# Add residual and RMSNorm over 65,536 rows: four rows per partition and tile instead of two, scaling traced one tile late, last store in rows

## The chip, the cores and the metric

The kernel runs on one core of a Trainium2 chip; the other cores are idle. Times are device microseconds (us) of that core, medians over repeated executions. A profiled execution gives a span, which is about 2 us shorter than the time of the same run because it counts from the first to the last instruction.

A packet is one record of the DMA trace: here the contiguous run of one partition, moved by one of the core's 16 DMA engines. A load or store of a tile gives each engine 8 of them.

## The reference

The input is 32 x 2048 rows of 2048 float32 numbers (8 KiB a row); x, residual and output are 537 MB each.

```python
z = x + residual
rms = np.sqrt(np.mean(z ** 2, axis=-1, keepdims=True) + eps)
return (z / rms * gamma).astype(np.float32)
```

## The kernel before

A tile has 128 partitions with R rows each. The rows of one partition are neighbours in DRAM, so each partition of a tile is one contiguous run of R x 8 KiB. Loads go out on the sync queue, stores on the scalar queue; VectorE adds and scales, ScalarE squares with a running sum and takes the root. (Lines are left out here; the whole kernel follows.)

```python
R = 2
n_tiles = n_rows // (P * R)                                  # 256
x_t = x_f.rearrange("(n p r) m -> n p r m", p=P, r=R)        # r_t, o_t alike
gamma_tile = singles.tile([P, D], fp32)
nc.sync.dma_start(out=gamma_tile, in_=gamma.partition_broadcast(P))
xio = ctx.enter_context(tc.tile_pool(name="xio", bufs=6))
rio = ctx.enter_context(tc.tile_pool(name="rio", bufs=4))
for i in range(n_tiles):
    x_tile = xio.tile([P, R, D], fp32)
    r_tile = rio.tile([P, R, D], fp32)
    nc.sync.dma_start(out=x_tile, in_=x_t[i])
    nc.sync.dma_start(out=r_tile, in_=r_t[i])
    nc.vector.tensor_add(out=x_tile, in0=x_tile, in1=r_tile)             # L56
    for g in range(R):
        nc.scalar.activation(out=sq_junk, in_=x_tile[:, g, :], func=Square,
                             accum_out=ssq[:, g : g + 1])                # L61
    # ... rms = sqrt(ssq / D + eps) on ScalarE (L69), rstd = 1 / rms on VectorE (L77)
    for g in range(R):
        nc.vector.scalar_tensor_tensor(out=x_tile[:, g, :], in0=x_tile[:, g, :],
            scalar=rstd[:, g : g + 1], in1=gamma_tile, op0=mult, op1=mult)  # L80
    nc.scalar.dma_start(out=o_t[i], in_=x_tile)
```

Of the kernel before, what the change touches and what calls it, by code (L numbers as in the profile page):

```python
# [1 line left out]

# [4 lines left out]


@with_exitstack  # L10
def kernel(
    ctx: ExitStack,
    tc: tile.TileContext,
    x: bass.AP,
    residual: bass.AP,
    gamma: bass.AP,
    eps: float,
    out: bass.AP,
):
    nc = tc.nc  # L20
    P = nc.NUM_PARTITIONS
    fp32 = mybir.dt.float32

    x_f = x.flatten_outer_dims()
    r_f = residual.flatten_outer_dims()
    o_f = out.flatten_outer_dims()

    n_rows, D = x_f.shape
    R = 2
    assert n_rows % (P * R) == 0  # L30
    n_tiles = n_rows // (P * R)

    x_t = x_f.rearrange("(n p r) m -> n p r m", p=P, r=R)
    r_t = r_f.rearrange("(n p r) m -> n p r m", p=P, r=R)
    o_t = o_f.rearrange("(n p r) m -> n p r m", p=P, r=R)

    inv_d = 1.0 / float(D)

    singles = ctx.enter_context(tc.tile_pool(name="singles", bufs=1))
    gamma_tile = singles.tile([P, D], fp32)  # L40
    nc.sync.dma_start(out=gamma_tile, in_=gamma.partition_broadcast(P))  # L41
    eps_tile = singles.tile([P, 1], fp32)
    nc.vector.memset(eps_tile, float(eps))  # L43

    xio = ctx.enter_context(tc.tile_pool(name="xio", bufs=6))
    rio = ctx.enter_context(tc.tile_pool(name="rio", bufs=4))
    stats = ctx.enter_context(tc.tile_pool(name="stats", bufs=8))
    psum = ctx.enter_context(tc.tile_pool(name="psum", bufs=1, space=bass.MemoryType.PSUM))

    for i in range(n_tiles):  # L50
        x_tile = xio.tile([P, R, D], fp32)
        r_tile = rio.tile([P, R, D], fp32)
        nc.sync.dma_start(out=x_tile, in_=x_t[i])  # L53
        nc.sync.dma_start(out=r_tile, in_=r_t[i])  # L54

        nc.vector.tensor_add(out=x_tile, in0=x_tile, in1=r_tile)  # L56

        sq_junk = psum.tile([P, D], fp32)
        ssq = stats.tile([P, R], fp32)
        for g in range(R):  # L60
            nc.scalar.activation(  # L61
                out=sq_junk,
                in_=x_tile[:, g, :],
                func=mybir.ActivationFunctionType.Square,
                accum_out=ssq[:, g : g + 1],
            )

        rms = stats.tile([P, R], fp32)
        nc.scalar.activation(  # L69
            out=rms,  # L70
            in_=ssq,
            func=mybir.ActivationFunctionType.Sqrt,
            bias=eps_tile,
            scale=inv_d,
        )
        rstd = stats.tile([P, R], fp32)
        nc.vector.reciprocal(out=rstd, in_=rms)  # L77

        for g in range(R):
            nc.vector.scalar_tensor_tensor(  # L80
                out=x_tile[:, g, :],
                in0=x_tile[:, g, :],
                scalar=rstd[:, g : g + 1],
                in1=gamma_tile,
                op0=mybir.AluOpType.mult,
                op1=mybir.AluOpType.mult,
            )

        nc.scalar.dma_start(out=o_t[i], in_=x_tile)


# [1 line left out]
_INS = ['x', 'residual', 'gamma', 'eps']  # L93
_OUTS = [((32, 2048, 2048), 'float32')]
#: Inputs that are plain numbers.
_NUMBERS = {'eps': 9.999999974752427e-07}


# [26 lines left out]
```

## Time and profile before

| quantity | value | where it is read |
|---|---|---|
| time, median | 3764.7 us (3764.1 to 3765.1) | runs |
| VectorE, ScalarE busy | 62%, 29% | profile page, part 1 |
| DMA busy share; rate | 9 (90% or more) nearly everywhere; 430 to 431 GB/s | page, part 2 |
| usual 16 KiB packet: lasts; start to start on one engine | 611 ns; 607.5 ns | DMA records |
| last load landed; from there to the end of the span | 3740.5 us; 22.0 us | DMA records |

The page of the kernel before. Part 2 cuts the span into 40 slices: busy tenths for each engine and for the DMA engines, then GB/s. Part 3 lists the queues (q1 loads, q10 stores, q14 instruction fetches) with packets, MB and share of the 16 engines' time. Part 4 is the chain of waits that ended last. Part 5 lists groups of instructions: busy us, mean ns of one, and the engine's idle time just before them with what ended most of it.

```profile
span 3762.5 us, 4011 instructions
DVE 2322.1 (62%) x1025; ACT 1103.6 (29%) x1282; POOL 0.2 (0%) x4
...
DMA  9999999999999999999999999999999999999998
GB/s 416 431 430 431 431 430 431 430 431 430 430 431 431 430 431 431 431 431 430 431 431 430 431 431 431 430 431 431 430 431 430 431 431 430 431 430 431 430 431 356
DMA packets 110767, 1611.96 MB, mean 428 GB/s; under 512 B 12304, under 2 KB 12304, under 8 KB 12304
...
q14 instruction: 31, 0.25, 0.0%
...
DMA 91%; DVE 8%; issue 1%; SPq 0%; ACT 0%; DVEq 0%
...
L56 DVE TENSOR_TENSOR x_tile<-x_tile,r_tile 128x4096 f32<-128x4096 f32 x256 | 1132.0, 4422 | 1413.1 <-DMA r_tile<-in_residual_dram 1413.0
L61 ACT ACTIVATE sq_junk<-x_tile 128x2048 f32<-128x2048 f32 x512 | 963.3, 1881 | 2637.9 <-DVE x_tile L56 2629.9
L80 DVE SCALAR_TENSOR_TENSOR x_tile<-x_tile,rstd,gamma_tile 128x2048 f32<-128x2048 f32 x512 | 1181.4, 2349 | 9.1
```

The compute engines have room: VectorE stands still 1413 us waiting for residual loads, and the chain that ended last is DMA for 91% of the span. The DMA rows are full and the rate is flat except in the first and last slice. The rate is therefore what most of the time is made of, and it is a sum over packets.

### The profile page before, as it was taken

Reading aid. Unit: us, or ns where it says so; the run is one execution under the profiler, and the core shown is the slowest. Engines: PE = TensorE matmul, PEld = TensorE weight load, DVE = VectorE, ACT = ScalarE, POOL = GpSimd, SP = SyncE. Lnnn points to the kernel's source line nnn. Section 1 sums busy time; section 2 is a strip of 40 time slices with the busy share of each in tenths; the row PEclk is TensorE's granted clock in tenths of the full one; section 3 lists DMA queues with packets and bytes.
Section 4 is the critical chain, followed back from the end, with each engine's and each line's share of the span. In section 5 each row is a group of like instructions: output and inputs, shape, how many; then the busy total and the mean of one; then the engine's idle time right before and its main releaser. Section 6 shows DMA issues by size and latency. Waiting matters only on the chain.

```text
span 3762.5 us, 4011 instructions
## 1 busy us (share of the span) xinstructions
DVE 2322.1 (62%) x1025; ACT 1103.6 (29%) x1282; POOL 0.2 (0%) x4
## 2 busy tenths in 40 slices
DVE  5566656666566655666566655666556665566656
ACT  3232322323223232322323232232323222232322
POOL 0000000000000000000000000000000000000000
DMA  9999999999999999999999999999999999999998
GB/s 416 431 430 431 431 430 431 430 431 430 430 431 431 430 431 431 431 431 430 431 431 430 431 431 431 430 431 431 430 431 430 431 431 430 431 430 431 430 431 356
DMA packets 110767, 1611.96 MB, mean 428 GB/s; under 512 B 12304, under 2 KB 12304, under 8 KB 12304
## 3 DMA queue, kind: packets, MB, share of 16 engines
q1 hardware_dynamic: 73872, 1074.82, 66.9%
q10 hardware_dynamic: 36864, 536.89, 33.3%
q14 instruction: 31, 0.25, 0.0%
HBM read 1074.79 MB, written 536.87 MB: 428 GB/s over the span
## 4 chain that ended last, share of the span: by engine, by line
DMA 91%; DVE 8%; issue 1%; SPq 0%; ACT 0%; DVEq 0%
DMA r_tile<-in_residual_dram 53%; DMA x_tile<-in_x_dram 22%; DMA out_dram<-x_tile 15%; DVE x_tile L80 5%; DVE x_tile L56 3%; SPq L53 0%; ACT sq_junk L61 0%; DVE rstd L77 0%; DVEq L120 0%; SPq L54 0%; DVEq L56 0%; SPq L41 0%; ACT rms L69 0%
## 5 line engine op out<-in xcount | busy, mean ns | idle before, releaser
L56 DVE TENSOR_TENSOR x_tile<-x_tile,r_tile 128x4096 f32<-128x4096 f32 x256 | 1132.0, 4422 | 1413.1 <-DMA r_tile<-in_residual_dram 1413.0
L61 ACT ACTIVATE sq_junk<-x_tile 128x2048 f32<-128x2048 f32 x512 | 963.3, 1881 | 2637.9 <-DVE x_tile L56 2629.9
L80 DVE SCALAR_TENSOR_TENSOR x_tile<-x_tile,rstd,gamma_tile 128x2048 f32<-128x2048 f32 x512 | 1181.4, 2349 | 9.1
L61 ACT ACTIVATION_READ_ACCUMULATOR sq_junk<-x_tile 128x1 f32 x512 | 95.4, 186 | 0.0
L69 ACT ACTIVATE rms<-ssq,eps_tile 128x2 f32<-128x2 f32 x256 | 75.7, 296 | 8.2
L77 DVE RECIPROCAL rstd<-rms 128x2 f32<-128x2 f32 x256 | 40.3, 158 | 10.1 <-ACT rms L69 10.1
L61 ACT ACT_TABLE_LOAD x1 | 1.3, 1283 | 0.7 <-PEq L106 0.7
L69 ACT ACT_TABLE_LOAD x1 | 1.3, 1283 | 0.0
L43 DVE MEMSET eps_tile<- 128x1 f32 x1 | 0.1, 59 | 0.8 <-PEq L106 0.8
L106 POOL MEMSET const-uint8-127<- 128x1 uint8 x1 | 0.1, 102 | 0.0
L106 POOL MEMSET const-bfloat16-1.0<- 128x1 bf16 x1 | 0.1, 101 | 0.0
L106 POOL MEMSET const-float32-0.0<- 128x1 f32 x1 | 0.1, 98 | 0.2 <-issue 0.2
L106 POOL MEMSET const-float32-1.0<- 128x1 f32 x1 | 0.1, 98 | 0.0
## 6 DMA issues: line engine op xcount, KB each, us to landing
x_tile<-in_x_dram SPq DMA_DIRECT2D x256, 2048.0 KB, 34.3
r_tile<-in_residual_dram SPq DMA_DIRECT2D x256, 2048.0 KB, 37.3
out_dram<-x_tile ACTq DMA_DIRECT2D x256, 2048.0 KB, 14.4
gamma_tile<-in_gamma_dram SPq DMA_DIRECT2D x1, 1024.0 KB, 4.3
```

The source lines that it names most:

```text
L43: nc.vector.memset(eps_tile, float(eps))
L56: nc.vector.tensor_add(out=x_tile, in0=x_tile, in1=r_tile)
L61: nc.scalar.activation(out=sq_junk, in_=x_tile[:, g, :], func=mybir.ActivationFunctionType.Square, accum_out=ssq[:, g : g + 1],)
L69: nc.scalar.activation(out=rms, in_=ssq, func=mybir.ActivationFunctionType.Sqrt, bias=eps_tile, scale=inv_d,)
L77: nc.vector.reciprocal(out=rstd, in_=rms)
L80: nc.vector.scalar_tensor_tensor(out=x_tile[:, g, :], in0=x_tile[:, g, :], scalar=rstd[:, g : g + 1], in1=gamma_tile, op0=mybir.AluOpType. ...
L106: nc = _bacc.Bacc("TRN2", target_bir_lowering=False, num_devices=1)
```

## The change

Its intent: half as many packets of twice the size, cheaper loading of gamma (four DMAs of one row, then copied across the partitions on chip, instead of a 1 MB broadcast from DRAM), scaling traced after the next tile's squares so that VectorE need not wait for them, and a last store in four rows so that each can leave as soon as it is scaled. The buffers for x and residual grow in bytes, from ten of 16 KiB per partition to six of 32 KiB (160 to 192 KiB), but in number they fall from 6 and 4 to 4 and 2.

```diff
-    R = 2
+    R = 4
-    nc.sync.dma_start(out=gamma_tile, in_=gamma.partition_broadcast(P))
-    xio = ctx.enter_context(tc.tile_pool(name="xio", bufs=6))
-    rio = ctx.enter_context(tc.tile_pool(name="rio", bufs=4))
-    stats = ctx.enter_context(tc.tile_pool(name="stats", bufs=8))
+    zio = ctx.enter_context(tc.tile_pool(name="zio", bufs=4))
+    rio = ctx.enter_context(tc.tile_pool(name="rio", bufs=2))
+    stats = ctx.enter_context(tc.tile_pool(name="stats", bufs=3))
     # ... load(i), reduce(i) (add, squares, root) and scale(i) hold the same
     # operations as before; x_tile is called z
+    def scale(i, z, rms, pieces):
+        # ... reciprocal, R scalings
+        n = R // pieces
+        for g in range(0, R, n):
+            nc.scalar.dma_start(out=o_t[i][:, g : g + n, :], in_=z[:, g : g + n, :])
+    def load_gamma():
+        nc.vector.memset(gamma_tile, 0.0)
+        for q in range(4):
+            nc.scalar.dma_start(
+                out=gamma_tile[32 * q : 32 * q + 1, :], in_=gamma.partition_broadcast(1)
+            )
+        nc.vector.stream_shuffle(gamma_tile, gamma_tile, [0] * 32)
+    load_gamma()
+    before = None
+    for i in range(n_tiles):
+        z, r_tile = load(i)
+        rms = reduce(i, z, r_tile)
+        if before is not None:
+            scale(i - 1, *before, 1)
+        before = (z, rms)
+    scale(n_tiles - 1, *before, R)
```

## The prediction

> **What bounds the kernel now.** The DMA engines. The page's slices show DMA at 9 (90% or more) almost everywhere and 430-431 GB/s in all but the first (416) and last (356). VectorE is busy 62%, ScalarE 29%; VectorE idles 1413 us waiting for the residual load (view of waits); the chain that ended last is 91% DMA. Only bytes, cost per packet and the two ends are worth time.
>
> The Trainium skill, "DMA: Bandwidth & Descriptors", section "Where 436 GB/s comes from", puts the ceiling at 435.2 GB/s. The trace agrees: 431 sustained, 1% below. The 1610.6 MB of x, residual and output can't get under 3701 us, so no change of schedule gives 2%.
>
> **What is left, from the packet records.** A 16 KiB packet takes 611 ns and the next on its engine starts 3 ns before it ends: period 608. An 8 KiB packet (gamma) takes 309, period 306. So: about 302 ns per 8 KiB plus 4 ns fixed. A DMA gives each of 16 engines 8 packets and one completion write (about 6 ns net): 8 x 608 + 6 = 4.87 us, x768 = 3740 us of the 3762.5 us span. The rest: 3 us of head; 2.4 us for gamma (1 MB); about 9 us by which three engines trail (at the end 81 GB/s, three sixteenths of the rate, goes on loading for 9 us; I put it to 31 instruction fetches of 8 KiB, those in the loop each followed by a packet of 970-1270 ns); about 7 us idle before the last store.
>
> **What the change does.**
> - 32 KiB packets: estimated period 4 x 302 + 4 = 1212 ns. A DMA is 8 x 1212 + 6 = 9.70 us, x384 = 3725.6 us. Saves 15 us, all on the critical path.
> - Gamma: four 8 KiB rows instead of 1 MB saves 2 us; its memset and shuffle run while the first tile loads.
> - A quarter fewer instructions, so fewer fetches: saves 2 us of trailing.
> - Deferred scaling: nothing in the loop. The cycle per tile is 29 us; VectorE needs 8.8 + 0.2 + 4 x 2.35 = 18.4, ScalarE 9. With two residual and four x buffers the next residual and x loads can be issued about 9 us after a residual lands, while 8 MB (over 19 us) of loads are still outstanding: no starvation.
> - Tail: worse. After the last load: add 8.8, the scaling of the tile before 9.5, only then the next-to-last store [...]; the store before it has run out 5 us after that landing. About 15 us of idle DMA against 7; then 8 MB of stores at full rate, the last rows hidden behind them. Costs 8 us.
>
> Sum: 3764.7 - 15 - 2 - 2 + 8 = about 3753.
>
> **Prediction: 3753 us, range 3742 to 3767.** Faster by over 2%: 1%; within 2%: 97%; slower by over 2%: 2%.
>
> **What would show each step.** 32 KiB packets at a 1212 ns period, a steady 432 GB/s; VectorE waiting only on the residual load; DMA at 9 in all middle slices; the last slice below 356 GB/s; about 23 fetches; 40 us from last load landing to end (22 before).
>
> **What would make it wrong.** 32 KiB rows split into 16 KiB packets (then about 3767); a larger stride between the engines' addresses slowing reads; residual loads issued too late with two buffers (gaps in the DMA rows); a larger fixed cost per packet than two sizes show (then below 3745).

## More of the kernel before

The end of the kernel before, by the view of windows. Columns: window, its length, busy time and count on DVE, ACT and POOL, granted clock, DMA share, GB/s.

```profile
3740.00:3749.00 9.00, 6.05 (x2) 2.88 (x3) 0.00 (x0) 1.00 0.86 366
3750.00:3756.00 6.00, 4.78 (x3) 0.42 (x3) 0.00 (x0) 1.00 0.00 0
3757.00:3761.00 4.00, 0.00 (x0) 0.00 (x0) 0.00 (x0) 1.00 0.93 393
```

And VectorE's timeline there (start us, length us, engine, line, operation, what it made; in brackets the idle time before it).

```profile
3727.84 4.42 DVE L56 TENSOR_TENSOR x_tile<-x_tile,r_tile 128x4096 f32<-128x4096 f32 x1 [8.00 <-DMA r_tile<-in_residual_dram]
3732.19 0.16 DVE L77 RECIPROCAL rstd<-rms 128x2 f32<-128x2 f32 x1
3732.38 4.62 DVE L80 SCALAR_TENSOR_TENSOR x_tile<-x_tile,rstd,gamma_tile 128x2048 f32<-128x2048 f32 x2
3736.91 0.16 DVE L77 RECIPROCAL rstd<-rms 128x2 f32<-128x2 f32 x1
3737.11 4.62 DVE L80 SCALAR_TENSOR_TENSOR x_tile<-x_tile,rstd,gamma_tile 128x2048 f32<-128x2048 f32 x2
3741.64 4.42 DVE L56 TENSOR_TENSOR x_tile<-x_tile,r_tile 128x4096 f32<-128x4096 f32 x1
```

Two things are to be seen. From 3750 to 3756 us no DMA moves a byte: the last tile is added, squared and scaled with nothing to store (the DMA records put this gap at 6.4 us). And the order on VectorE is not the order of the source: it is two additions, then the scaling of both tiles. The kernel as built already works in pairs of tiles, because instructions are reordered when the program is built.

The experiments ran in three groups on three chips (e1 to e4 on chip 13, f1 to f4 on chip 2, g1 to g4 on chip 3), each with the kernel before beside it.

## The result, and the profile after

The changed kernel took 3742.8 us (four runs: 3741.55, 3741.64, 3743.96, 3756.69) against 3764.65 us (3764.07 to 3765.12). The ratio is 0.9951, with a 95% interval of 0.9935 to 0.9966: within 2%, and a real gain of about half a per cent. Ratios here are the mean time of one kernel's runs over that of the other's from the same rounds, so they are not quite the ratio of the medians that I quote. All outputs are right.

The page after, in the same parts.

```profile
span 3742.0 us, 2813 instructions
DVE 2292.4 (61%) x772; ACT 1066.4 (28%) x1154; POOL 0.2 (0%) x4
...
DMA  9999999999999999999999999999999999999998
GB/s 420 432 435 432 432 433 435 432 432 433 434 432 432 434 433 432 432 434 433 432 432 435 432 432 433 433 433 432 434 432 432 433 434 432 433 434 433 431 433 350
DMA packets 55757, 1610.84 MB, mean 430 GB/s; under 512 B 6196, under 2 KB 6196, under 8 KB 6196
...
q14 instruction: 21, 0.17, 0.0%
...
DMA 67%; DVE 16%; issue 14%; another core or an unknown queue 1%; ACT 0%; DVEq 0%; SPq 0%
...
L64 DVE TENSOR_TENSOR z<-z,r_tile 128x8192 f32<-128x8192 f32 x128 | 1112.1, 8689 | 1407.4 <-issue 1052.8
L67 ACT ACTIVATE sq_junk<-z 128x2048 f32<-128x2048 f32 x512 | 963.3, 1881 | 2652.2 <-DVE z L64 2640.1
L78 DVE SCALAR_TENSOR_TENSOR z<-z,rstd,gamma_tile 128x2048 f32<-128x2048 f32 x512 | 1170.0, 2348 | 4.5
```

The compute work for one row is nearly the same (squares 1881 ns in both, scaling 2349 against 2348 ns; an addition of four rows takes 8689 ns, of two rows 4422 ns), VectorE's idle time before the additions is the same (1407 against 1413 us), and every middle slice of the rate has gone up by 1 to 5 GB/s with half the packets. So the gain is not in the work of the compute engines; the rate is what changed. (The page puts most of VectorE's idle time to "issue" now, and the chain is DMA for 67% where it was 91%. This only means that it found no releaser for 46 of the 65 waits; the other 19 have the residual load.) The view of waits of the changed kernel says this in two lines: who waited for what, us in total, times, the longest.

```profile
DVE z L64 <- issue: 1052.8, 46, 25.4
DVE z L64 <- DMA r_tile<-in_residual_dram: 354.7, 19, 23.9
```

The end of the changed kernel by windows, with the same columns as before.

```profile
3710.00:3721.00 11.00, 8.68 (x2) 2.26 (x3) 0.00 (x0) 1.00 1.00 429
3722.00:3730.00 8.00, 2.79 (x3) 5.05 (x7) 0.00 (x0) 1.00 0.00 0
3731.00:3740.00 9.00, 5.53 (x3) 0.00 (x0) 0.00 (x0) 1.00 1.00 413
```

And VectorE's timeline at that end.

```profile
3682.86 8.69 DVE L64 TENSOR_TENSOR z<-z,r_tile 128x8192 f32<-128x8192 f32 x1 [24.80 <-issue]
3691.47 0.17 DVE L76 RECIPROCAL rstd<-rms 128x4 f32<-128x4 f32 x1
3691.67 9.14 DVE L78 SCALAR_TENSOR_TENSOR z<-z,rstd,gamma_tile 128x2048 f32<-128x2048 f32 x4
3700.73 0.17 DVE L76 RECIPROCAL rstd<-rms 128x4 f32<-128x4 f32 x1
3700.93 9.14 DVE L78 SCALAR_TENSOR_TENSOR z<-z,rstd,gamma_tile 128x2048 f32<-128x2048 f32 x4
3709.99 8.69 DVE L64 TENSOR_TENSOR z<-z,r_tile 128x8192 f32<-128x8192 f32 x1
3727.18 0.18 DVE L76 RECIPROCAL rstd<-rms 128x4 f32<-128x4 f32 x1 [8.50 <-ACT rms L71]
```

Again additions and scalings come in pairs, although the source alternates them. The store of the next-to-last tile was issued before the last addition began, at 3710 us, and kept the engines busy until 3721.6 us. The gap without any DMA is then 9.0 us (3721.6 to 3730.6), not the 15 us that I had predicted from the order of the source.

Where 20.5 us of span went (3762.5 to 3742.0), from the DMA records of the two profiles, per engine and averaged over 16 engines:

| part | before | after | difference | predicted |
|---|---|---|---|---|
| engine busy, in all | 3744.2 | 3723.2 | -21.0 | -19 |
| of which the tiles' packets at their usual period | 3736.9 | 3718.7 | -18.2 | -15 |
| of which gamma's packets | 2.4 | under 0.1 | -2.4 | -2 |
| of which the rest (worked out) | | | about -0.4 | -2 |
| idle in the last 100 us | 14.4 | 15.6 | +1.2 | +8 |
| idle in between | 0.6 | 0.0 | -0.6 | 0 |

The second line is 768 DMAs x (8 x 607.49 + 5.9) ns before, and 384 x (8 x 1209.76 + 5.9) ns after: the mean time from the start of one undelayed packet to the start of the next on its engine, and about 5.9 ns for the completion record that ends each engine's part of a DMA. The busy line is measured from merged records of which some 0.3% could not be assigned to an engine without doubt, which may put a few us of error on its level and less on the difference; the differences add up to the 20.5 us of the span.

### The profile page after: what moved, and what is told of

It reads as the page before. It is cut to its first block, busy times and chain, and to the rows that moved or that the text cites. A ratio compares the mean times of both kernels' runs of the same rounds, so it can differ in the third digit from the quotient of the medians.

```text
span 3742.0 us, 2813 instructions
## 1 busy us (share of the span) xinstructions
DVE 2292.4 (61%) x772; ACT 1066.4 (28%) x1154; POOL 0.2 (0%) x4
## 4 chain that ended last, share of the span: by engine, by line
DMA 67%; DVE 16%; issue 14%; another core or an unknown queue 1%; ACT 0%; DVEq 0%; SPq 0%
DMA out_dram<-z 28%; DMA z<-in_x_dram 28%; DMA r_tile<-in_residual_dram 11%; DVE z L78 9%; DVE z L64 8%; ACT sq_junk L67 0%; DVE rstd L76 0%; DVEq L138 0%; SPq L59 0%; ACT L71 0%; ACT rms L71 0%; DVEq L64 0%; SPq L60 0%
## 5 line engine op out<-in xcount | busy, mean ns | idle before, releaser
L64 DVE TENSOR_TENSOR z<-z,r_tile 128x8192 f32<-128x8192 f32 x128 | 1112.1, 8689 | 1407.4 <-issue 1052.8
L67 ACT ACTIVATE sq_junk<-z 128x2048 f32<-128x2048 f32 x512 | 963.3, 1881 | 2652.2 <-DVE z L64 2640.1
L78 DVE SCALAR_TENSOR_TENSOR z<-z,rstd,gamma_tile 128x2048 f32<-128x2048 f32 x512 | 1170.0, 2348 | 4.5
L67 ACT ACTIVATION_READ_ACCUMULATOR sq_junk<-z 128x1 f32 x512 | 95.8, 187 | 0.0
L71 ACT ACTIVATE rms<-ssq,eps_tile 128x4 f32<-128x4 f32 x128 | 38.1, 298 | 4.1
L76 DVE RECIPROCAL rstd<-rms 128x4 f32<-128x4 f32 x128 | 21.9, 171 | 18.3 <-ACT rms L71 18.3
L97 DVE LOAD_MASK_SELECT gamma_tile<-gamma_tile x1 | 0.0, 14 | 12.7 <-DMA gamma_tile<-in_gamma_dram 12.7
## 6 DMA issues: line engine op xcount, KB each, us to landing
z<-in_x_dram SPq DMA_DIRECT2D x128, 4096.0 KB, 32.2
```

What stands on the lines that cost most here:

```text
L64: nc.vector.tensor_add(out=z, in0=z, in1=r_tile)
L67: nc.scalar.activation(out=sq_junk, in_=z[:, g, :], func=Act.Square, accum_out=ssq[:, g : g + 1])
L71: nc.scalar.activation(out=rms, in_=ssq, func=Act.Sqrt, bias=eps_tile, scale=inv_d)
L76: nc.vector.reciprocal(out=rstd, in_=rms)
L78: nc.vector.scalar_tensor_tensor(out=z[:, g, :], in0=z[:, g, :], scalar=rstd[:, g : g + 1], in1=gamma_tile, op0=mult, op1=mult,)
L97: nc.vector.stream_shuffle(gamma_tile, gamma_tile, [0] * 32)
```

## The experiments

Theory A: the gain is the number of packets. Each packet costs its bytes and a small fixed time, and the bytes didn't change. Rival B: the gain comes from the schedule (the deferred scaling, the reordered buffers). Rival C: it comes from the ends (gamma, the last store in rows). The second question came with the repetition of the changed kernel: why the times of one program scatter.

In the tables, "stalls" is the time by which load and store packets outlast their usual length (309, 611 or 1213 ns for 8, 16 or 32 KiB), per engine over the profiled run. The kernel before, run beside each group, had a median of 3764.2 to 3764.3 us every time.

### e1: the changed kernel again, unedited

> The changed kernel again, unaltered, for more rounds: one of its first four runs took 3756.7 us and the others 3741.6 to 3744.0. If the long run was a rare disturbance, five more runs lie at 3740 to 3745 us. If the kernel has two modes (for example because its pairs of stores and loads fall into a bad phase), one or two of five lie near 3755, and a profile of such a run should show a steady rate below 432 GB/s or DMA idle in the middle.

Measured: 3742.8, 3744.0, 3744.3, 3753.8, 3764.6 and 3767.3 us, all at clock 1.000; ratio 0.9963 [0.9945, 0.9981]. With the four runs before, that is ten runs of one program: six from 3741.6 to 3744.3, and four from 3753.8 to 3767.3 us, median 3744.2. All runs of the kernel before lie within 2 us of each other. So the change has a short mode, a group of six within 3 us, and a long one; the four long runs scatter over 14 us and are not a second fixed time. Both kinds came up among six runs on one chip. The profiled run happened to be long (span 3762.6 us), which lets the two be compared. The rates by windows, first for the short profile (the one shown as the result above); GB/s is the last column:

```profile
100.00:900.00 800.00, 482.59 (x160) 224.87 (x244) 0.00 (x0) 1.00 1.00 433
1100.00:3600.00 2500.00, 1534.80 (x517) 714.75 (x774) 0.00 (x0) 1.00 1.00 433
```

The same windows of e1, the long profile:

```profile
100.00:900.00 800.00, 480.95 (x158) 224.28 (x243) 0.00 (x0) 1.00 1.00 433
1100.00:3600.00 2500.00, 1521.08 (x510) 710.74 (x770) 0.00 (x0) 1.00 1.00 431
```

The long run begins like the short one and slows down after about 900 us. The DMA share is 1.00 in both: in these windows the lost time isn't idle time but packets that take longer. They outlast their usual length by 19.8 us per engine against 4.7 us. Of the 20.6 us between the two spans, 15.0 are busy time, 4.8 idle time in the last 100 us and 0.7 idle time in between.

### e3 and e4: the changed kernel with two or four DMAs per tile

```diff
-        nc.sync.dma_start(out=z, in_=x_t[i])
-        nc.sync.dma_start(out=r_tile, in_=r_t[i])
+        for g in range(0, R, n):     # n = 2 in e3 (16 KiB packets), 1 in e4 (8 KiB)
+            nc.sync.dma_start(out=z[:, g : g + n, :], in_=x_t[i][:, g : g + n, :])
+        for g in range(0, R, n):
+            nc.sync.dma_start(out=r_tile[:, g : g + n, :], in_=r_t[i][:, g : g + n, :])
...
-            scale(i - 1, *before, 1)
+            scale(i - 1, *before, 2)     # 4 in e4
```

> The changed kernel with every load and store of a tile cut into two transfers of two rows each; tiles, buffers, arithmetic and traced order as in the changed kernel. Only the packets go from 32 KiB to 16 KiB and the transfers double. My theory: 768 x (8 x 608 + 6 ns) = 3740.2 us of DMA work per engine instead of 384 x (8 x 1210 + 6) = 3719.4, so 21 us longer than the changed kernel, near 3764 us. Rival (tile size and schedule give the gain, not the packets): within 4 us of the changed kernel, near 3743.

> The same with four transfers of one row each: packets of 8 KiB. My theory, from the 306 ns period of an 8 KiB packet: 1536 x (8 x 306 + 6 ns) = 3769.3 us, 50 us longer than the changed kernel, near 3793 us, in line with 8 KiB, 16 KiB and 32 KiB packets all costing 5 to 6 ns fixed. Rival (the gain comes from the schedule): near 3743.

| kernel | time | ratio to before | usual period of a packet | idle in between |
|---|---|---|---|---|
| changed, 32 KiB packets | 3744.2 (short mode about 3742) | 0.9951, 0.9963 | 1209.8 ns | 0.0 us |
| e3, 16 KiB | 3766.1 (3765.3 to 3766.4) | 1.0004 [0.9992, 1.0016] | 607.5 ns | 0.5 us |
| e4, 8 KiB | 3824.6 (3820.8 to 3826.4) | 1.0159 [1.0146, 1.0172] | 306.1 ns | about 4 us |

e3 keeps the tiles, the buffers, the gamma and the last store in rows of the change and halves the packets. The whole gain is gone, and 18.2 us of it by the packets' period alone. But the edit did one thing more: in its built program VectorE alternates additions and scalings where the change takes them in pairs, and the idle time at the end is 18.7 us against 15.6. g1 below halves the packets and keeps the pairs. The page of e3 has the flat rate of the kernel before:

```profile
GB/s 415 431 430 431 431 431 431 430 430 431 431 431 431 430 431 431 431 431 431 431 431 431 431 430 431 431 430 430 432 430 431 431 431 430 431 430 431 431 430 336
```

Three sizes give the fixed cost of a packet: 2 x 306.13 - 607.49 = 4.8 ns, and 2 x 607.49 - 1209.76 = 5.2 ns. From 16 to 32 KiB a run saves 384 x 8 x 5.2 ns = 16 us of these per engine, and 384 completion records of 5.9 ns, together the 18.2 us of the table above. The Trainium skill ("DMA: Bandwidth & Descriptors", section "Why small descriptors are slow (HBM only)") gives a fixed overhead of about 3 cycles per packet; at the 850 MHz of its section "Where 436 GB/s comes from" this would be an estimated 3.5 ns. The trace has a fixed term too, of 5 ns; that it is the same one isn't shown. That section stresses descriptors of 256 bytes; the runs show that at 16 KiB a fixed term still is half a per cent of a kernel that does nothing but move bytes.

e4 went further up than packets explain: 1536 x (8 x 306.13 + 5.9) ns is 34 us more work than e3 has, and it took 58 us more. It ran at 426 to 427 GB/s for the first 1400 us, which the period explains (8 x 8192 B x 16 in 2.455 us is 427 GB/s), and then dropped to between 419 and 426, with longer packets: they outlast their usual length by 33.5 us per engine, against 7.0 us in e3, which makes up the rest (about 4 us were idle in between). This is the second question again, and the expectation (near 3793 us) missed by 32 us for this reason.

### g1: the changed kernel with two rows per tile and as many bytes of buffers

```diff
-    R = 4
+    R = 2
-    zio = ctx.enter_context(tc.tile_pool(name="zio", bufs=4))
-    rio = ctx.enter_context(tc.tile_pool(name="rio", bufs=2))
-    stats = ctx.enter_context(tc.tile_pool(name="stats", bufs=3))
+    zio = ctx.enter_context(tc.tile_pool(name="zio", bufs=8))
+    rio = ctx.enter_context(tc.tile_pool(name="rio", bufs=4))
+    stats = ctx.enter_context(tc.tile_pool(name="stats", bufs=6))
```

> The changed kernel with 2 rows per tile again and twice the buffers (eight x, four residual): traced order, narrow gamma load, last store in rows and buffer bytes as in the change, packets of 16 KiB as before. My theory: DMA work 3740.2 us per engine as before, gamma saves 2.4 us, the smaller last tile about 2 us in the tail: about 3760 us, all rounds within 2 us of each other, loads averaging under 613 ns. Rival (the change's other parts carry the gain): 3745 us or less.

Measured: 3760.1 us (3759.9 to 3760.6), ratio 0.9989 [0.9976, 1.0002] (the interval just reaches 1, but no run of the one overlaps the runs of the other); no long mode in five runs. VectorE's order is in pairs, as in the change and in the kernel before, so this is the cleanest test of packet size. At two rows, everything of the change but the four rows is worth 4.2 us: 2.4 us of gamma, and about 2 us at the end (idle per engine in the last 100 us 12.3 against 14.4 us). This is all that rivals B and C get at two rows; at four rows the store in rows is worth more, because it keeps the end from growing (f4). The four rows are worth the remaining 16 us of the short mode: 18.9 us less busy time than g1, and 3.3 us more idle time at the end.

### e2: the kernel before with four rows, four x and two residual buffers

```diff
-    R = 2
+    R = 4
-    xio = ctx.enter_context(tc.tile_pool(name="xio", bufs=6))
-    rio = ctx.enter_context(tc.tile_pool(name="rio", bufs=4))
+    xio = ctx.enter_context(tc.tile_pool(name="xio", bufs=4))
+    rio = ctx.enter_context(tc.tile_pool(name="rio", bufs=2))
```

> The kernel before with only the rows per partition raised from 2 to 4 and the buffers set to four x and two residual; wide gamma load, traced order and whole last store as before. My theory (packet size is the gain, the tail takes part of it back): packets of 1210 ns period save 20.8 us, fewer instruction fetches about 2, the tail costs about 13 us more than before because the program's last pair of adds stands before the last pair of scalings, so about 20 us pass without DMA work: about 3755 us. Rival (the new order of scaling and the last store in rows are the gain): within 3 us of 3764.6.

Measured: 3775.9 us (3770.8 to 3781.5), ratio 1.0032 [1.0020, 1.0044]: slower than before, with the same 32 KiB packets, and 21 us above what I had expected (3755). The records say where the packets' gain went. First, stalls: 21.8 us per engine against 6.8 in the kernel before, so that the busy time is only 1.4 us less instead of 18 us. Second, the end: 29.2 us idle in the last 100 us against 14.4, with one gap of 19.4 us without any DMA. The last slice of its page shows it (290 GB/s, against 356 before and 350 after).

```profile
DMA  9999999999999999999999999999999999999996
GB/s 421 432 427 431 432 433 428 433 429 433 427 430 433 430 432 431 429 430 429 432 432 430 431 433 432 433 431 430 430 432 428 433 429 431 431 431 427 430 431 290
```

The end depends on where the pairs fall. In the built order of e2 the first two tiles stand alone, so the last two of 128 are a pair: both are added before either is scaled, and no store is under way while the last tile is added and squared. In the change one tile stands alone at the start, and the last tile is left alone behind a full pair. The kernel before, undeferred with 256 tiles, ends the same way, so deferral isn't needed for it; with four rows it is what e2 and the change differ in here. Nothing else that the deferral does was seen. The single GB/s figures of the middle slices (427 to 433) also show the stalls: the slices are no longer even.

### f1 and f2: order and size exchanged

The scheduler's order was fixed with fences that hold back reordering and add no work to the engines (VectorE 772 and ScalarE 1154 instructions in f1, as in the change). f1 is the change with 32 KiB packets in strictly alternating order (add i, scale i-1); f2 is e3's 16 KiB packets in the pairs of the change.

```diff
# f1
         rms = reduce(i, z, r_tile)
+        tc.no_sync_barrier()
         if before is not None:
             scale(i - 1, *before, 1)
+            tc.no_sync_barrier()
# f2: loads as in e3, and
+        waiting.append((i, z, reduce(i, z, r_tile)))
+        if i % 2 == 0 or i == n_tiles - 1:
+            tc.no_sync_barrier()
+            for j, zj, rms in waiting:
+                scale(j, zj, rms, R if j == n_tiles - 1 else 2)
+            tc.no_sync_barrier()
+            waiting = []
```

> The changed kernel with fences for the scheduler so that VectorE really runs in the traced order (add of tile i, then scaling of tile i-1); without them the built program pairs them (two adds, then eight row scalings, then two stores back to back), as the built kernel before did with its smaller tiles. Packets of 32 KiB. In the repeat run of the changed kernel, loads stalled about 0.5 us at a time at a fixed place in the cycle of two tiles, some 15 us per engine in all. If the pairing (8 MB of loads and of stores issued at once) brings the stalls, this run has none: all rounds within 3 us of each other, loads averaging under 1216 ns, at about 3748 us (3742 plus some 6 us for the longer idle gap that the traced order leaves in the tail, 15 us against 9.5). If packets of 32 KiB bring them whatever the order, the rounds scatter as before, by 10 to 25 us.

> Packets of 16 KiB as in the run with two transfers per tile, but with fences that force the paired order of the built changed kernel. If pairing brings the stalls: loads average clearly over the 612.6 ns of the undisturbed 16 KiB runs, rounds scatter, 3765 to 3790 us. If the packet size brings them: none, about 3764 us, all rounds within 2 us of each other.

| | 16 KiB packets | 32 KiB packets |
|---|---|---|
| alternating | e3: 3766.1 (3765.3 to 3766.4) | f1: 3762.1 (3752.9 to 3792.5), ratio 1.0008 [0.9982, 1.0034] |
| in pairs | f2: 3796.7 (3796.3 to 3797.3), ratio 1.0086 [1.0073, 1.0099] | the change: 3744.2 (3741.6 to 3767.3) |

The order alone doesn't give the gain: f2 has the pairs of the change and is 30 us slower than e3, since the packets of its stores outlast their usual length by 37.1 us per engine. Pairs as such don't cost that, for the kernel before and g1 have pairs and 16 KiB packets too, with 0.4 and 0.5 us; why f2 stalls was not found, and neither of its two forecasts held (its rounds agree within about 1 us, at 3797). The table mixes two chips as well: f1 and f2 ran on chip 2, e3 and the repeats of the change on chip 13. The kernel before took the same time on both, but the change was never run on chip 2, so what a chip does to the stalls is not known. Alternation doesn't cure the scatter: f1 spreads over 40 us, more than the change. Its profiled run (3758.7 us) had 9.4 us of stalls in loads and 7.8 us in stores, and a gap of 15.6 us at the end, the one that I had predicted for the change: with this order the scaling of the tile before does stand between the last addition and the next-to-last store.

### f4: the change with its last store whole

```diff
-    scale(n_tiles - 1, *before, R)
+    scale(n_tiles - 1, *before, 1)
```

> The changed kernel with the last tile stored in one piece instead of rows. In the profile of the changed kernel the first row's store is issued at 3729.8 us and the last row's scaling ends about 3736.5 us, so the last 4 MB start about 6.8 us later: 6 to 7 us longer between the start of the last scaling and the end (14.6 us in the changed kernel). Stalls of loads may hide it in the times; in the profile the tail shows it. Rival (the rows only trade one long store for four starts): under 2 us.

Measured: 3772.4 us (3772.3 to 3773.3), ratio 1.0022 [1.0009, 1.0035]. The gap at the end is 15.6 us instead of 9.0 us: 6.6 us longer, because the store goes out when all four rows are scaled (line L78: 9.14 us) and not after the first. VectorE's and the scalar queue's timeline of f4:

```profile
3750.03 9.14 DVE L78 SCALAR_TENSOR_TENSOR z<-z,rstd,gamma_tile 128x2048 f32<-128x2048 f32 x4
3759.20 0.34 ACTq L88 DMA_DIRECT2D out_dram<-z  x1
```

and of the change, where the first of four stores starts 2.4 us after the scaling does:

```profile
3727.39 9.14 DVE L78 SCALAR_TENSOR_TENSOR z<-z,rstd,gamma_tile 128x2048 f32<-128x2048 f32 x4
3729.77 7.13 ACTq L88 DMA_DIRECT2D out_dram<-z  x4
```

The store in rows is worth those 6.6 us. Most of the rest looks like the long mode: the profile of f4 has 19.9 us of stalls (15.8 in loads, 4.1 in stores), as e1's has 19.8, and its span is 8.8 us longer than e1's (3771.4 and 3762.6), with 9.3 us more idle time in the last 100 us. All four runs of f4 agree within about 1 us, although its loop is that of the change, which ran long in four of ten. But those six repeats were on another chip; whether chip 2 alone makes this loop run long is untested.

### f3 and g4: a shorter end

Both load the last residual in four DMAs of one row and add, square, scale and store the last tile row by row. f3 does it behind the alternating loop of f1; g4 behind the change's own loop, with fences only after it.

```diff
-    for i in range(n_tiles):
+    for i in range(n_tiles - 1):
...
-    scale(n_tiles - 1, *before, R)
+    scale(n_tiles - 2, *before, 1)
+    tc.no_sync_barrier()
+    # ... last tile: x in one DMA, the residual in four, then per row
+    #     add, square, root; reciprocal, scale, store on the sync queue,
+    #     in the order A0 A1 s0 A2 s1 A3 s2 s3
```

> The fenced traced order, with the tail made to keep the DMA engines busy: the next-to-last tile is scaled before the last one is added, and the last tile is loaded (residual), added, squared, scaled and stored row by row. By my account of the tail the stores of the two tiles before give the engines 14 us of work after the last load lands, and the last tile's first rows need less, so there is no idle gap: about 10 to 15 us shorter than the fenced kernel without it and 8 to 10 us shorter than the changed kernel at its best, near 3733 us if no loads stall.

> The changed kernel (its own order in the loop) with only the last tile changed: residual loaded in rows, then added, squared, scaled and stored row by row. In the changed kernel the DMA engines are idle for about 8 us between the end of the two stores before and the first row of the last tile. That gap goes: about 8 us less than the changed kernel in the same mode, 3734 us at its best, and the same scatter upwards of 10 to 25 us where loads stall, since the loop is untouched.

In both the gap at the end fell to 1.0 us, as intended. f3 took 3771.0 us (3768.8 to 3780.5), ratio 1.0026 [1.0013, 1.0039], for its loop had 34.7 us of stalls; I had expected 3733 us if no loads stalled. g4 took 3736.2, 3736.4, 3745.6, 3754.4, 3759.2 and 3761.1 us; median 3750.0, ratio 0.9958 [0.9939, 0.9978]. Its best is the best time of the study, 5.4 us below the change's best. But its times scatter as those of the change do, here without a clear break between short and long, and the medians (3750.0, against 3749.0 for the six runs of e1 and 3744.2 for all ten runs of the change) don't show it to be better. (g4 ran on chip 3, e1 on chip 13.) Page of g4's profiled run, a short one:

```profile
span 3734.6 us, 2825 instructions
...
GB/s 420 432 432 432 432 433 435 432 433 432 432 432 433 432 432 433 434 433 433 432 433 432 433 432 433 434 433 433 433 433 432 433 432 433 432 434 433 433 433 385
```

The last slice is 385 GB/s instead of 350: the idle time per engine in the last 100 us fell from 15.6 to 7.5 us.

### g2: the kernel before with four x and two residual buffers of two rows

If the stalls come from too few loads in the queue, the kernel before should stall too with few and small buffers.

```diff
-    xio = ctx.enter_context(tc.tile_pool(name="xio", bufs=6))
-    rio = ctx.enter_context(tc.tile_pool(name="rio", bufs=4))
+    xio = ctx.enter_context(tc.tile_pool(name="xio", bufs=4))
+    rio = ctx.enter_context(tc.tile_pool(name="rio", bufs=2))
```

> The kernel before, 2 rows per tile, with four x and two residual buffers (the counts of the changed kernel, so half its bytes). Three or so engines fall behind the others by up to 12 us over the run [...], and a buffer is free only when its slowest engine is done. If it is the depth of the buffers in time, not the packet size, that lets engines run out of loads, then here too the fastest engine has under 5 us of loads left when a store arrives (17 to 24 us in the kernel before), packets get longer in places (load average over 614 ns), and the time rises by 10 us or more, to 3775 to 3830. If only 32 KiB or 8 KiB packets bring the stalls: within 3 us of 3764.2.

Measured: 3768.2 us (3767.1 to 3771.3), ratio 1.0011 [0.9999, 1.0023]. Stalls in loads rose by 6.3 us (6.4 to 12.7 us per engine) and the time by 4 us, partly given back by a shorter idle time at the end (10.5 against 14.4 us). So the stalls are no matter of large packets alone, but the effect was smaller than I expected.

### g3: the kernel before with idle GpSimd instructions, for more instruction fetches

```diff
+    idle_tile = singles.tile([P, 1], fp32)
...
+        for _ in range(32):
+            nc.gpsimd.tensor_copy(out=idle_tile, in_=rms[:, 0:1])
```

> The kernel before with 8192 one-element copies added on the idle GpSimd, 32 per tile, so some 64 more instruction fetches of 8 KiB (31 before); the time of the copies themselves is hidden. If a fetch costs a DMA engine about 0.8 us (0.3 for itself and 0.5 on the packet after it) and the fetches of one engine's program all fall on one DMA engine, that engine has 50 us more work, falls behind until the buffers run out at some 20 us and then sets the pace: 3764 + 30 to 45 us, near 3800, with a last-to-first spread of landings over 20 us early in the run. If fetches spread over all 16 engines: 3 to 4 us more, near 3768. If they cost nothing: 3764.

This experiment failed. Fetches rose from 31 to 100, but GpSimd became the bottleneck (438 ns for each of 8192 copies; with the pauses between them they fill the whole span), and the kernel took 4113.9 us, ratio 1.0928. It says nothing about fetches.

```profile
DMA  9999999999999999999999999999999999999991
GB/s 417 430 431 430 430 430 431 400 395 391 392 401 393 390 392 396 399 392 390 395 401 393 390 392 397 397 395 395 389 397 396 388 396 394 396 397 387 397 398 67
...
q14 instruction: 100, 0.81, 0.1%
...
L79 POOL COPY idle_tile<-rms 128x1 f32<-128x1 f32 x8192 | 3588.5, 438 | 522.4 <-ACT rms L71 25.0
```

It does teach how to read the DMA row: the DMAs were short of work here, and the row still shows 9 throughout while the rate fell to 394 GB/s. The load packets lasted 650 ns on average, against 613 ns in the kernel before. Here a part of the DMAs' slack showed as longer packets, and the busy share hid it.

### What the records say of the stalls

For each profile I followed how long the fastest engine still had loads to do when a store was issued (the margin), and how often an engine had run out of loads when the next one came.

| profile | stalls in loads, stores (us per engine) | margin: lowest tenth, median (us) | ran out of loads |
|---|---|---|---|
| before | 6.4, 0.4 | 19.4, 25.7 | 0 of 471 |
| change, short mode | 4.2, 0.5 | 23.3, 28.1 | 13 of 236 (16 us in sum) |
| g4, short mode | 4.6, 0.5 | 22.3, 27.1 | 19 of 236 (38 us) |
| e3 | 6.5, 0.5 | 25.1, 28.6 | 0 |
| g1 | 6.5, 0.5 | 20.5, 26.0 | 0 |
| change, long mode (e1) | 18.4, 1.4 | 7.9, 11.1 | 46 of 235 (606 us) |
| f4 | 15.8, 4.1 | 11.1, 20.4 | 45 of 235 (320 us) |
| e2 | 18.8, 3.0 | 8.4, 11.9 | 52 of 236 (648 us) |
| g2 | 12.7, 0.6 | 11.0, 12.4 | 92 of 472 (235 us) |
| f2 | 6.0, 37.1 | 1.4, 1.8 | 59 of 466 (406 us) |
| f1 | 9.4, 7.8 | 27.4, 32.2 | 1 of 238 |

These counts follow the single engines through merged records, so small ones are uncertain; a coarser count from the loads' completion records gives nearly the same numbers of lapses, with smaller sums.

Most of these profiles fit one story, which is argued from the records and was not isolated by an experiment: loads come too late for the engine that is furthest ahead. A load counts as landed when its slowest engine has finished. The Trainium skill says so ("DMA: Bandwidth & Descriptors", section "Why a DMA increments its semaphore by 16 and not by 1": the engines finish independently, and only the full 16 mean that all data has landed), and the trace agrees: each load has 16 completion records, and over the whole run the last of them comes a median 7.5 us after the first in the short profile and 15.4 us in the long one (in the last twelfth at the most 15.5 and 32.8 us). In the kernel before this grows from 1.3 us in the first twelfth of the run to 15.2 us in the last, and it doesn't stall: its margin is large enough for it. The next load waits for a buffer, which waits for an addition, which waits for that last engine. By this account an engine that trails holds back new work for those that lead. In the long profile 559 packets of 32 KiB take over 200 ns longer than usual, and 357 of them start within 4 us after a store was issued, at the same place in the cycle of two tiles (58.4 us).

f1 doesn't fit: it stalled with a large margin. f2 fits only in part: its engines land within a median 0.8 us of each other, so none trails, and its lost time is in the stores. f3, which is not in the table, stalled by 34.7 us with lapses of about 40 us in sum by the coarser count, where e1 has over 550. So too few loads can't be the only cause. f1, f2 and f3 all ran on chip 2. What sends a run of one program into the short or the long mode was not found; it is left open.

## Why the prediction was right

Within 2% and the range (3742 to 3767) held; the median of the first four runs, 3742.8 us, is at the range's low edge, and the ten runs together, 3741.6 to 3767.3 us, fill it and reach just past both ends. Within 2% was safe, since the prediction's own bound of 3701 us leaves 1.7%. That the median fell inside the range owed something to luck: two errors, of 3 and 7 us, went the same way and left it 0.8 us from the edge, and the scatter upwards was not foreseen. The mechanism of the gain (fewer packets at a fixed cost each) was right. Terms of the sum were mis-sized, and one statement was wrong.

- **The limit.** Right. The rate in the middle is 432.9 GB/s (432 predicted), 430.6 before; no other edit than larger packets raised it (g1, with all the rest of the change, has 430.6). The ceiling of 435.2 GB/s that the prediction took from the Trainium skill was not exceeded: no slice of the pages shown is above 435 GB/s.
- **Packets: -15 us predicted, -18.2 measured.** I had put the fixed part at 4 ns from two sizes rounded to nanoseconds, and the 32 KiB period at 1212 ns. It is 5.2 ns and 1209.8 ns. Over 3072 packets per engine those 2 ns are 7 us; the period before, 607.5 instead of 608 ns, takes 3 of them back. g1 shows the term by itself, e3 nearly so.
- **Gamma: -2 predicted, -2.4 measured.** Right.
- **Fetches: -2 predicted.** Their number was nearly right (23 predicted, 21 measured). That they make engines trail was read from the records only; the experiment for it failed, so the term is neither shown nor refuted. The rest in the table, about -0.4 us, is smaller than the possible error of the busy time.
- **The end: +8 predicted, +1.2 measured.** This is the largest mis-sized term. The prediction read the order of the source ("add 8.8, the scaling of the tile before 9.5, only then the next-to-last store"); in the built program the next-to-last store goes before the last addition, and the gap is 9.0 us, not 15, against 6.4. f1 shows the predicted gap once the order is that of the source. A smaller part: I had taken 2 us from a store's issue to its first byte, and the trace shows 0.8 us (3729.77 to 3730.6). For a load it is 1.0 us at the run's start (0.73 to 1.74), of which the issuing instruction itself is about 0.4. The Trainium skill (same page, section "Latency and other measured facts") has about 600 ns to the first byte, which was nearer than my figure.
- **"No starvation": wrong in some runs.** The prediction compared the bytes outstanding (over 19 us of loads) with the time until new loads are issued, as if all engines moved in step. In the short mode that was good enough: 13 short lapses of 16 us in sum. In the long mode loads ran out 46 times and the run is 10 to 25 us longer. This looks like the "residual loads issued too late" of its last paragraph, though the cause is open (see above); it shows as long packets, not as the gaps in the DMA row that it named.
- **The signs in the profile.** DMA at 9 in all middle slices, a last slice below 356 (350), 40 us from the last load's landing to the end (39.9; 22.0 before): all as predicted. They were weak tests. The long mode has the same row of nines, and 40 us came out right for a wrong reason: 31 of them were stores and 9 a gap, where I had counted 25 and 15.

## What to carry to other kernels

When a kernel is bound by moving bytes and its DMA row is full, the contiguous run per partition is still a lever: doubling it from 16 to 32 KiB saved a fixed 5 ns per packet, 18 us of 3762. It has to be weighed against having fewer buffers (g2: with fewer of them the kernel before stalled 6.3 us more) and against a longer end (e2: 15 us). Read the order of instructions from the timeline of the built program and not from the source before you cost a change of schedule, above all at the end. Repeat a kernel that is fast once, and repeat the reference kernel of an experiment on the same chip: here runs of one program lay up to 26 us apart, more than the whole change was worth.

## What the Trainium skill lacked or had wrong

- "DMA: Bandwidth & Descriptors", section "Why small descriptors are slow (HBM only)": about 3 cycles fixed per packet, an estimated 3.5 ns at 850 MHz. Three sizes of packets give 4.8 and 5.2 ns here, and a completion record of 5.9 ns for each engine and DMA.
- The same page, "Rules for kernel authors": 1 MiB or more per DMA for the most bandwidth. Here DMAs of 1, 2 and 4 MiB all satisfy it, and the changed kernel ran at 3824.6, 3766.1 and 3744.2 us with them. The length of the run per partition (8, 16, 32 KiB) changed with the size of the DMA; by the periods above, packets and completion records explain 34 of the 58 us between the first two times and 18 of the 22 us between the last two.
- The same page, the warning in "Where 436 GB/s comes from", lets the HBM side bind transfers between HBM and SBUF at about 358 GB/s. A core alone moved 430.6 to 432.9 GB/s here, two thirds of it reads. "HBM Reference", section "Specifications (TRN2)", has about 425 GB/s for a core alone, which is much nearer, and lower than these runs.
- No page has what an instruction fetch costs the data packets on the DMA engines: 31 of them in the run before (8 KiB each), all in the loop, each followed by a packet of 970 to 1270 ns instead of 611.
- No page says that packets can last longer where DMAs are short of work: in g3 load packets averaged 650 ns instead of 613, and the rate fell to 394 GB/s with 9 in every middle slice of the DMA row.
- No page has the scatter: one program took about 3742 us or up to 3767 us from run to run at the same clock, with packets outlasting their usual length by 4.7 or 19.8 us per engine in the two runs profiled. Its cause is open.
